# Stores of the early stages issued by GpSimd instead of SyncE in a one-core encoder layer

## The chip, the cores and the metric

The kernel runs on one core of a Trainium2 chip. A core has a tensor engine (TensorE, PE in the profile), a vector engine (VectorE, DVE), a scalar engine (ScalarE, ACT), GpSimd (POOL) and SyncE (SP), which here does nothing but issue transfers. Each engine runs its own instructions in order, and they wait for each other through semaphores. Transfers between the core's memory and the chip's large memory are carried by 16 DMA engines; an engine that issues a transfer writes it into its own queue and goes on, and whoever needs the data waits for its landing. The metric is the time of one execution in microseconds on the device, as the median of several.

## The reference

One layer of a bidirectional encoder, batch 1, 1024 rows, width 2048, in fp32:

```
mod = silu(c) @ w_ada + b_ada;  shift, scale, gate = split(mod, 3)
h = rmsnorm(x, pre_g) * (1 + scale) + shift
q, k, v, gate_a, u, gate_p = split(h @ w_in)           # 1024, 256, 256, 1024, 1024, 1024 columns
y_a = windowed_gqa(q, k, v, rel_table, sink) * silu(gate_a)   # 8 heads of 128, window of 128
y_p = multiscale_pool(u, w_grp, scale) * silu(gate_p)         # 4 groups, windows 2, 4, 8, 16
g_a, g_p = split(sigmoid(h @ w_merge + b_merge))
merged = g_a * (y_a @ w_br_attn) + g_p * (y_p @ w_br_pool)
out = x + gate * rmsnorm(merged @ w_out, post_g)
```

## The kernel before, in words

Every large product is fp32, made of three products of halves: ACT rounds a tile to its high part (`whi`, L96) and VectorE subtracts that to get the low part (`wlo`, L97). On top of that `strassen` (L213 on) saves one product in eight: a block of 2x2 tiles is computed with seven products, named by their moving operands B11, T3, T2, B21, T4, T1, B22, into three PSUM banks X, Z and V (TensorE's L238). Each product is 12 matmuls. Its weight halves live in rings of four tiles, so weights are prepared up to four products ahead. The seventh product of a block runs after the first two of the next block's. The results of a block are called c (two tiles), u2 and p7; the tiles named `ev` or `part` they stand in are free again once the store that reads them has landed. A block's inner dimension is done in two halves, and the sums of the first half travel through the large memory.

The stages, in order of time:

- Start-up, to about 60 us: x is normalized and turned, and parts of `w_ada` come in, column by column, for shift and scale.
- The ramp: five blocks over smaller pieces of the inner dimension. The first of them is written as a plain product (`plain_block`, stores at L665 into `ramp_d0`). Their results go to `ramp_d` and come back as `part` (L210).
- Pass one, the first half of the inner dimension for `w_in` and `w_merge`: c, u2 and p7 are stored to `part_d` by `to_dram` (L315). Beside it run sums of weights for the last stage (`weight_sums`: loads `sw` at L795, sums on VectorE, stores to `ws_d` at L807), the lines of the attention's bias (`bias_lines`, L828 to L838: `oh`, `line_d`, `bias_d`, always issued by GpSimd) and the gate's row (`pg_d`, L867).
- Pass two, the second half: parts are loaded from `part_d` (L210), added, and the results stored to `proj_d` (L315). Beside it run the attention (loads of `qr`, `kvr`, `g` from `proj_d`, stores of `ya_d` at L1085) and the pooling (`yp_d`, L1177).
- The merge: two branches b = 0 and b = 1, eight blocks each. Branch 0 stores its results to `mp_d` (L1306); branch 1 adds them and stores `m_d` (L1311). The gate tiles `gt` come from `proj_d` (L1271).
- The output projection with row tiles of its own; first row tiles are stored by GpSimd (`o_d` at L1443, `out_dram` at L1371 through `first_rows`), the last ones by SyncE (`finish_block`, L1371).

The order of instructions on each engine is set by a scheduler that works from its own estimates, except where `keep` pins an instruction to its place in the program. Before the change SyncE's one queue holds the loads and 445 stores, in one order: a store whose result isn't ready yet holds up every load behind it. A queue has eight transfers under way at most, since it uses eight completion semaphores in turn.

Two names of the code are touched: `load` and `store`, set side by side, and the default of `finish_block`.

Of the kernel before, what the change touches and what calls it, by code (L numbers as in the profile page):

```python
# [43 lines left out]
def encoder_layer(ctx: ExitStack, tc: tile.TileContext, x, c, table, w_ada, b_ada, pre_g,  # L44
# [15 lines left out]
    nc = tc.nc  # L60
# [30 lines left out]
    def keep(ins):  # L91

        tc.keep_in_program_order(ins)
# [12 lines left out]
        return nc.vector.tensor_tensor(o, a, b, ALU.subtract)  # L106

    load = nc.sync.dma_start
    store = nc.sync.dma_start

    ident = const.tile([P, P], F32, name="ident")
    make_identity(nc, ident)
# [243 lines left out]
    for r0, src in ((0, c[0]), (16, b_ada[0, 0:D]), (32, b_ada[0, D:2 * D]),  # L356
                    (48, pre_g[0]), (64, b_merge[0]), (96, pool_scale[0])):
        n = src.shape[0] // P
# [996 lines left out]
    def rows_of(T, n):  # L1355
        return out[T * P:(T + 1) * P, n * 512:(n + 1) * 512]
# [8 lines left out]
        nc.vector.reciprocal(s_[:, 2:3], s_[:, 1:2])  # L1365
        return s_[:, 2:3]

    def finish_block(T, n, scale, store=store):
        r = held.pop((T, n))
        keep(nc.vector.scalar_tensor_tensor(r, r, scale, xrow.pop((T, n)), op0=ALU.mult, op1=ALU.add))  # L1370
        store(rows_of(T, n), r)  # L1371
# [11 lines left out]
    def out_pair(half, i, op, between, after=None):  # L1383
# [101 lines left out]
        for t in range(2):  # L1485
            for j, w in enumerate(ws):
                out_mm(bz[t], op, "B22", j, t, w, False, j == len(ws) - 1)
            result("12", t, bz[t], c12[t])
            scale = row_scale(6 + t)
            for n in (0, 2, 3, 1):  # L1490
                finish_block(6 + t, n, scale)
# [7 lines left out]
    def first_rows(T, n):  # L1499

        def place(name):
            ring.rotate(-1)
            return ring[-1]

        def fetch():
            if (T, n) not in held:
                held[T, n] = place("fo")
                keep(load(held[T, n], o_d[T * P:(T + 1) * P, n * 512:(n + 1) * 512]))
            fetch_x_block(T, n, place)

        def put_out():
            if T not in scales:
                scales[T] = row_scale(T)
            finish_block(T, n, scales[T], nc.gpsimd.dma_start)

        return fetch, put_out
# [53 lines left out]
    def third_block():  # L1570
        assert not side
        for T in (4, 5):
            scale = row_scale(T)
            for b in range(4):
                finish_block(T, b, scale)
# [43 lines left out]
```

## Time and profile before

| | |
|---|---|
| median of three executions | 2119.83 us (2118.78 to 2121.57) |
| the profiled execution | 2119.98 us, span 2118.2 us |
| TensorE busy, granted clock | 2083.7 us, 98% of the span; 0.997 |
| VectorE, ACT, GpSimd busy | 1541.5 us (73%), 1108.4 us (52%), 20.1 us (1%) |
| moved by SyncE's queue | 457.82 MB, 66.1% of the time of 16 DMA engines |
| moved by GpSimd's queue | 8.48 MB, 1.0% |

The page gives the busy time of each engine and the chain of work that ended last. A row of the view of waits names the engine, its operation and source line, then the engine that released it; after the colon stand the microseconds in total, how often, and the longest. A row of the timeline gives the start, the length, the engine, line and tiles. A row of the view of busy time by stretch gives the stretch, its length, the busy time of TensorE (and how many instructions), of its weight loads, of VectorE, ACT and GpSimd, the granted clock, the share of the DMA engines and GB/s. `SPq` is SyncE's sequencer. A row of DMA issues ends with the size in KB and the median time from issue to landing.

### The profile page before, as it was taken

The numbers are of one execution on the slowest core, as the hardware profiler recorded it, in microseconds if no ns is written. First come the engines' busy times: TensorE is split into PE (matmuls) and PEld (weight loads), VectorE is DVE, ScalarE is ACT, GpSimd is POOL, SyncE is SP. The second block draws the span as 40 slices with busy tenths as digits, with TensorE's granted clock in tenths as the row PEclk, the third lists the DMA queues.
The fourth block names the chain that finished last, engine by engine and source line by source line (L and its number), as shares of the span: only waits on it lengthen the run. The fifth ranks groups of instructions, "written<-read, shape, count | busy, mean of one in ns | idle before, by whom it ended". The sixth has DMA issues, their size and how long they took to land.

```text
span 2118.2 us, 29001 instructions
## 1 busy us (share of the span) xinstructions
PE 2083.7 (98%) x9573; PEld 1715.9 (81%) x9573; DVE 1541.5 (73%) x2767; ACT 1108.4 (52%) x2106; POOL 20.1 (1%) x90
## 2 busy tenths in 40 slices
PE   6999999999999999999999999999999999999998
PEld 4688888888887888888888888888888788888886
DVE  5787667777546776677777678866957977889667
ACT  4654444444366544665656544333645645768654
POOL 0000000000000000000000000000000000000000
PEclk9999999999999999999999999999999999999999
DMA  9887656899767456544645476676745566786896
GB/s 332 276 267 229 204 190 212 290 307 324 252 194 238 148 178 200 169 159 161 198 145 168 154 240 226 211 225 197 250 155 173 173 195 197 225 307 218 299 342 214
DMA packets 302934, 468.20 MB, mean 221 GB/s; under 512 B 24074, under 2 KB 145058, under 8 KB 302784
## 3 DMA queue, kind: packets, MB, share of 16 engines
q1 hardware_dynamic: 299408, 457.82, 66.1%
q0 software_dynamic: 3040, 8.48, 1.0%
q8 instruction: 75, 1.23, 0.2%
q14 instruction: 75, 0.61, 0.1%
q10 hardware_dynamic: 336, 0.06, 0.0%
HBM read 341.45 MB, written 126.90 MB: 221 GB/s over the span
## 4 chain that ended last, share of the span: by engine, by line
PE 92%; DVE 4%; DMA 3%; issue 1%; ACT 0%; SPq 0%; ACTq 0%; DVEq 0%
PE Z L238 31%; PE X L238 20%; PE V L238 20%; PE Z L1349 2%; PE Z L1351 2%; PE Z L1350 2%; PE X L1351 1%; PE X L1349 1%; PE X L1350 1%; PE V L1349 1%; PE V L1351 1%; PE V L1350 1%; DMA ada<-in_w_ada_dram 1%; PE PT L1060 1%; DVE wlo L97 1%; DMA xt<-in_x_dram 1%
## 5 line engine op out<-in xcount | busy, mean ns | idle before, releaser
L96 ACT ACTIVATE whi<-raw 128x512 fp32r<-128x512 f32 (+1 forms) x532 | 322.0, 606 | 515.9 <-PE Z L238 255.1
L97 DVE TENSOR_TENSOR wlo<-raw,whi 128x512 fp32r<-128x512 f32 (+1 forms) x532 | 347.1, 657 | 164.7 <-PE Z L238 125.2
L97 DVE TENSOR_TENSOR wlo<-wr,whi 128x512 fp32r<-128x512 f32 x224 | 151.3, 689 | 56.5 <-ACT whi L96 51.1
L96 ACT ACTIVATE whi<-wr 128x512 fp32r<-128x512 f32 x224 | 138.9, 629 | 89.0 <-DVE wlo L97 37.2
L103 DVE TENSOR_TENSOR raw<-raw,raw 128x512 f32<-128x512 f32 x79 | 54.6, 691 | 104.5 <-DMA raw<-in_w_merge_dram 78.8
L238 PE MATMUL V<-T3h,whi 128*128 128x512 f32 x334 | 91.4, 392 | 1.5 <-DVE u L103 1.0
L96 ACT ACTIVATE whi<-ws 128x512 fp32r<-128x512 f32 (+1 forms) x88 | 53.5, 608 | 74.5 <-PE X L238 68.2
L238 PE MATMUL Z<-T2h,whi 128*128 128x512 f32 x334 | 91.1, 392 | 0.5 <-ACT whi L96 0.5
L238 PE MATMUL X<-B11h,whi 128*128 128x512 f32 x334 | 91.3, 392 | 0.0
L238 PE MATMUL Z<-T1h,whi 128*128 128x512 f32 x334 | 91.3, 391 | 0.0
L238 PE MATMUL Z<-T2h,wlo 128*128 128x512 f32 x334 | 90.3, 390 | 1.0 <-DVE wlo L97 1.0
L238 PE MATMUL Z<-B22h,whi 128*128 128x512 f32 x334 | 91.1, 392 | 0.0
L238 PE MATMUL V<-T4l,whi 128*128 128x512 f32 x334 | 90.7, 390 | 0.3 <-DVE T4l L97 0.2
L238 PE MATMUL X<-B21h,whi 128*128 128x512 f32 x334 | 90.7, 391 | 0.0
L238 PE MATMUL V<-T3l,whi 128*128 128x512 f32 x334 | 90.4, 390 | 0.2 <-DVE T3l L97 0.2
L238 PE MATMUL V<-T4h,whi 128*128 128x512 f32 x334 | 90.6, 391 | 0.0
L238 PE MATMUL Z<-T1l,whi 128*128 128x512 f32 x334 | 90.4, 390 | 0.1
L238 PE MATMUL X<-B11l,whi 128*128 128x512 f32 x334 | 90.4, 390 | 0.0
L238 PE MATMUL X<-B11h,wlo 128*128 128x512 f32 x334 | 90.3, 390 | 0.0
L238 PE MATMUL Z<-T1h,wlo 128*128 128x512 f32 x334 | 90.2, 390 | 0.0
L238 PE MATMUL Z<-B22l,whi 128*128 128x512 f32 x334 | 90.2, 390 | 0.0
L238 PE MATMUL X<-B21l,whi 128*128 128x512 f32 x334 | 90.2, 389 | 0.0
(353 smaller groups left out, 4838.3 us busy)
## 6 DMA issues: line engine op xcount, KB each, us to landing
part<-part_d SPq DMA_DIRECT2D x136, 256.0 KB, 4.7
ada<-in_w_ada_dram SPq DMA_DIRECT2D x128, 256.0 KB, 5.3
raw<-in_w_merge_dram SPq DMA_DIRECT2D x64, 512.0 KB, 5.5
wr<-ws_dS SPq DMA_DIRECT2D x64, 512.0 KB, 5.3
raw<-in_w_in_dram SPq DMA_DIRECT2D x62, 512.0 KB, 4.1
wr<-in_w_out_dram SPq DMA_DIRECT2D x48, 512.0 KB, 5.6
proj_d<-part SPq DMA_DIRECT2D x68, 256.0 KB, 2.2
sw<-in_w_out_dram SPq DMA_DIRECT2D x64, 256.0 KB, 5.8
```

What stands on the lines that cost most here:

```text
L96: ins = (nc.scalar.activation(hi, src, AF.Copy), nc.vector.tensor_tensor(lo, src, f32(hi), ALU.subtract))
L97: nc.vector.tensor_tensor(lo, src, f32(hi), ALU.subtract))
L103: return (eng or nc.vector).tensor_tensor(o, a, b, ALU.add)
L238: nc.tensor.matmul(ps, w_[:, i], op[mov][j][m_], start=fresh and i == 0 and n == 0, stop=i == nj - 1 and n == 2, skip_group_check=True)
L1060: nc.tensor.transpose(pt[:, i * P:(i + 1) * P], p[:, i * P:(i + 1) * P], ident)
L1349: nc.tensor.matmul(pb, hi, w[0], start=first, stop=False, skip_group_check=True)
L1350: nc.tensor.matmul(pb, lo, w[0], start=False, stop=False, skip_group_check=True)
L1351: nc.tensor.matmul(pb, hi, w[1], start=False, stop=last, skip_group_check=True)
```

## The change

The name `store`, which all stages use, becomes GpSimd's issue instead of SyncE's; `finish_block` keeps SyncE as its default.

```
@@ -106,7 +106,7 @@
     load = nc.sync.dma_start
-    store = nc.sync.dma_start
+    store = nc.gpsimd.dma_start
@@ -1365,7 +1365,7 @@
-    def finish_block(T, n, scale, store=store):
+    def finish_block(T, n, scale, store=nc.sync.dma_start):
```

So 429 stores leave SyncE's queue for GpSimd's: those at L315, L665, L807, L867, L1085, L1177, L1306 and L1311. GpSimd issues 456 transfers afterwards instead of 27. Every load that reads stored rows, and every tile that is reused after a store, still waits for the landing. The scheduler also places some instructions of the other engines anew: on TensorE it is 104 lines of difference in 9185 rows, the largest of which puts the products T2 and B21 of the block with bank Z_5318 ahead of its T3.

In the rows below a number behind a name tells buffers apart. First SyncE at the end of the start-up, before: `ada` are pieces of `w_ada`, `raw` weights of `w_in`, `ramp_d` with L665 the four stores of the plain block.

```order
L665 DMA ramp_d_86<-c_781 128x512
L471 DMA ada_413<-in_w_ada_dram 128x2x256
L188 DMA raw_415<-in_w_in_dram 128x2x256 x2
L188 DMA raw_418<-in_w_in_dram 128x2x256 x2
L665 DMA ramp_d_86<-c_786 128x512
L665 DMA ramp_d_86<-c_799 128x512
L665 DMA ramp_d_86<-c_804 128x512
L315 DMA ramp_d_87<-c_880 128x512
```

The same place on SyncE after the change:

```order
L471 DMA ada_411<-in_w_ada_dram 128x2x256
L471 DMA ada_413<-in_w_ada_dram 128x2x256
L188 DMA raw_415<-in_w_in_dram 128x2x256 x2
L188 DMA raw_418<-in_w_in_dram 128x2x256 x2
L188 DMA raw_1242<-in_w_in_dram 128x2x256 x2
L188 DMA raw_1245<-in_w_in_dram 128x2x256 x2
L188 DMA raw_1248<-in_w_in_dram 128x2x256 x2
L210 DMA part_1391<-ramp_d_87 128x512
```

The stores are gone from between the loads. On GpSimd they follow its last fill of a tile in the start-up:

```order
L549 MEMSET B22l_385 128x1
L665 DMA ramp_d_86<-c_781 128x512
L665 DMA ramp_d_86<-c_786 128x512
L665 DMA ramp_d_86<-c_799 128x512
L665 DMA ramp_d_86<-c_804 128x512
L315 DMA ramp_d_87<-c_880 128x512
```

All four stand there in a row, with nothing but their own results to wait for.

Second, GpSimd around the bias lines, before (`tab` is the table that `oh` selects from):

```order
L549 MEMSET B22l_385 128x1
L828 MEMSET tab 33x8
L831 DMA oh<-in_onehot_dram 33x512
L836 DMA line_d<-bl 8x512
L837 DMA bias_d<-line_d 1024x1x512
```

And after, from the store that stands ahead of `oh`:

```order
L315 DMA part_d<-p_1040_4836 128x512
L831 DMA oh<-in_onehot_dram 33x512
L836 DMA line_d<-bl 8x512
L315 DMA part_d<-c_5030 128x512
L837 DMA bias_d<-line_d 1024x1x512
L315 DMA part_d<-c_5084 128x512
L315 DMA part_d<-u_1080_5055 128x512
L315 DMA part_d<-p_1070_4997 128x512
L315 DMA part_d<-c_5199 128x512
L807 DMA ws_dS_98<-sw_5090 128x512
L315 DMA part_d<-c_5251 128x512
L807 DMA ws_dS_97<-sw_5202 128x512
```

The three transfers now stand among stores of pass one and of the weight sums.

Third, SyncE some 20 us later, before: `sw` are the loads for the weight sums, `xt` the last row tiles of x.

```order
L795 DMA sw_5259<-in_w_out_dram 128x512
L795 DMA sw_5261<-in_w_out_dram 128x512
L795 DMA sw_5263<-in_w_out_dram 128x512
L795 DMA sw_5265<-in_w_out_dram 128x512
L315 DMA part_d<-c_5199 128x512
L188 DMA raw_5381<-in_w_merge_dram 128x4x256
L315 DMA part_d<-c_5251 128x512
L315 DMA part_d<-u_1112_5233 128x512
L188 DMA raw_5383<-in_w_merge_dram 128x4x256
```

And after:

```order
L795 DMA sw_5259<-in_w_out_dram 128x512
L795 DMA sw_5261<-in_w_out_dram 128x512
L188 DMA raw_5381<-in_w_merge_dram 128x4x256
L188 DMA raw_5383<-in_w_merge_dram 128x4x256
L188 DMA raw_5565<-in_w_merge_dram 128x4x256
L795 DMA sw_5263<-in_w_out_dram 128x512
L795 DMA sw_5265<-in_w_out_dram 128x512
L188 DMA raw_5567<-in_w_merge_dram 128x4x256
L919 DMA xt_5539<-in_x_dram 128x512
```

Three loads of weights have moved ahead of the second half of the `sw` loads.

## The prediction

> **What bounds the kernel now.** I read the page first, its busy line and its chain of waits, and then TensorE's own waits.
>
> ```profile
> PE 2083.7 (98%) x9573; PEld 1715.9 (81%) x9573; DVE 1541.5 (73%) x2767; ACT 1108.4 (52%) x2106; POOL 20.1 (1%) x90
> PE 92%; DVE 4%; DMA 3%; issue 1%; ACT 0%; SPq 0%; ACTq 0%; DVEq 0%
> ```
>
> TensorE is busy for 98% of the span and carries 92% of the chain. A queue matters only where it makes TensorE stand. The view of busy time by stretch says how much standing there is after the start-up:
>
> ```profile
> 60.00:100.00 40.00, 37.20 (x190) 22.88 (x189) 30.18 (x68) 25.45 (x53) 0.00 (x0) 1.00 0.88 288
> 100.00:2080.00 1980.00, 1975.76 (x9025) 1640.85 (x9025) 1448.49 (x2556) 1036.91 (x1949) 16.50 (x44) 1.00 0.66 217
> ```
>
> Between 60 and 100 us TensorE stands 2.80 us, between 100 and 2080 us 4.24 us. So 7.0 us is the most that quicker loads could give back; the last 38 us keep their stores on SyncE. Nothing of that size limits a loss. Next, what SyncE's queue waited for:
>
> ```profile
> SPq L315 <- DVE part L103: 225.0, 53, 11.2
> SPq L315 <- ACT c L310: 177.1, 52, 7.1
> ```
>
> The two costliest rows are 402 us in which a store stood at the head of SyncE's queue for a result, with loads queued behind it. That is what the change takes away. It looks large, but only 7.0 us of standing was ever TensorE's.
>
> **The price of a store.** The change moves 429 stores, nearly all of 128x512 floats, to GpSimd. GpSimd already issues some of the same shape, so both prices stand in the trace (the view by source line, then the DMA issues with microseconds from issue to landing):
>
> ```profile
> L1371 POOL DMA_DIRECT2D out_dram<-mo x8: 539/540/542, 2014.0 to 2050.5; - x8
> L1371 SPq DMA_DIRECT2D out_dram<-mo x8: 332/332/351, 2096.6 to 2113.3; - x8
> ...
> proj_d<-part SPq DMA_DIRECT2D x68, 256.0 KB, 2.2
> mp_d<-c SPq DMA_DIRECT2D x16, 256.0 KB, 2.0
> out_dram<-mo POOLq DMA_DIRECT2D x8, 256.0 KB, 5.7
> out_dram<-mo SPq DMA_DIRECT2D x8, 256.0 KB, 2.3
> out_dram<-c POOLq DMA_DIRECT2D x2, 256.0 KB, 7.0
> oh<-in_onehot_dram POOLq DMA_DIRECT2D x1, 66.0 KB, 3.3
> ```
>
> Issue: 429 x 0.54 = 232 us of GpSimd, which is idle but for 20.1 us, so it costs nothing by itself. SyncE gets 429 x 0.33 = 142 us back, also free. Landing is what counts: 5.7 against 2.3 us, 3.4 us more for each store. I use 6 us for a landing from GpSimd. Whoever waits for a landing sees it later: a buffer that is reused, or a load that reads the stored rows back. Most have cover, because weights are prepared up to four products ahead and a product of 12 matmuls is 2.7 us (three groups of four that start 0.91 us apart; two of them, 802.97 to 804.78, stand under term 5). I walked the changed order against the times of before, looking for waits whose cover is under 3.4 us.
>
> [...]
>
> **Term 1, the head.** Up to 83 us the transfers are the bound. ACT has the four ramp_d0 tiles ready by 66.4 us, SyncE issues their stores between its loads, and VectorE then stands 6 us for the weight tile raw:
>
> ```profile
> L664 ACT ACTIVATE c<-PB x4: 595/601/608, 63.2 to 65.8; 128x512 f32<-128x512 f32 x4
> L665 SPq DMA_DIRECT2D ramp_d<-c x4: 319/338/343, 75.4 to 81.2; - x4
> 76.91 2.60 SPq L188 DMA_DIRECT2D raw<-in_w_in_dram  x4
> 79.81 1.68 SPq L665 DMA_DIRECT2D ramp_d<-c  x3
> DVE ws L106 <- DMA raw<-in_w_in_dram: 6.0, 1, 6.0
> 72.00:76.00 4.00, 4.00 (x26) 1.90 (x25) 1.48 (x4) 1.20 (x3) 0.00 (x0) 1.00 1.10 347
> 80.00:84.00 4.00, 3.45 (x22) 1.97 (x21) 1.02 (x3) 1.01 (x2) 0.00 (x0) 1.00 1.10 380
> ```
>
> Before, one of the four stores is ahead of raw and three are behind it. After, GpSimd has nothing else to do and issues all four at 64 to 67 us, so three more stores, 786 KB, pass the full engines before raw. At 347 GB/s that is 2.3 us; the mixed stretch ran at 380, which makes it a little less. If stores rode along wholly free it would be 0. I take +2.0, near the upper end, because 380 is nearer to 347 than to a rate that would carry them free. VectorE's sum behind raw moves by that, and TensorE, which already stands there (3.45 of 4 us busy), with it.
>
> **Term 2, the bias lines.** Before, GpSimd's queue holds these three alone. Afterwards the one-hot load oh stands behind a store of the seventh product, which is ready at 532.8 us:
>
> ```profile
> 532.81 0.32 SPq L315 DMA_DIRECT2D part_d<-p  x1
> 526.93 0.66 POOL L831 DMA_DIRECT2D oh<-in_onehot_dram  x1 [364.69 <-DMA raw<-in_w_merge_dram]
> 545.67 1.11 POOL L837 DMA_DIRECT2D bias_d<-line_d  x1 [5.08 <-DMA line_d<-bl]
> 538.12 1.02 PE L833 MATMUL b<-oh,tab 33*8 33x512 f32 x2
> ```
>
> oh leaves at 532.8 + 0.5 = 533.3 us and lands 3.3 us later, at 536.6, which is 1.5 us ahead of TensorE's use; if it takes a store's 6 us, TensorE waits 1.2. I take +0.5 (0 to 1.5). bias_d waits in GpSimd for line_d's landing, 5.1 us, with nine or more stores queued behind; they go out late by that, and stores of weight sums also wait behind one of ACT's c.
>
> **Term 3, the weight sums and the last row of x, 555 to 602 us.** In the changed order the loads sw_5263 and sw_5265 stand behind raw_5565. Before, they left in the burst of four that began at 554 us; raw_5565 left at 582.7:
>
> ```profile
> 554.13 8.91 SPq L795 DMA_DIRECT2D sw<-in_w_out_dram  x4
> 582.70 4.04 SPq L188 DMA_DIRECT2D raw<-in_w_merge_dram  x2
> 580.51 1.28 SPq L919 DMA_DIRECT2D xt<-in_x_dram  x3
> 583.75 1.34 ACT L920 ACTIVATE xt<-xt,rstd 128x512 f32<-128x512 f32 x2 [1.50 <-DMA xt<-in_x_dram]
> 600.59 0.60 PE L926 MATMUL b<-ident,xt 128*128 128x128 f32 x4
> sw<-in_w_out_dram SPq DMA_DIRECT2D x64, 256.0 KB, 5.8
> ```
>
> Step by step: sw at 583.2, landed at 589.0 (5.8); two sums on VectorE of 0.7 each, 590.4; the store from GpSimd landed at 596.4; xt reuses that buffer, loads 3.2 us as here (580.51 to 583.75), 599.6; scaled 0.7 later, 600.3. TensorE transposes xt at 600.6. So the 17 us of cover (583.75 to 600.59) are used up, and what is left is 0 to 2 us; I take +0.9. ACT stands some 6 us for it, but the next weights are not used before 603 us.
>
> **Term 4, the turn between the two branches.** c must be stored before ACT may write the seventh product's copy into its buffer:
>
> ```profile
> 1650.08 0.32 SPq L1306 DMA_DIRECT2D mp_d<-c  x1
> 1653.89 0.60 ACT L248 ACTIVATE p<-V 128x512 f32<-128x512 f32 x1 [0.23 <-PE V L238]
> 1658.42 0.61 ACT L96 ACTIVATE T4h<-y 128x512 fp32r<-128x512 f32 x1
> 1659.13 1.07 PE L238 MATMUL V<-T4h,whi 128*128 128x512 f32 x4
> 1640.00:1660.00 20.00, 20.00 (x88) 16.27 (x88) 19.87 (x34) 15.76 (x29) 0.00 (x0) 1.00 0.43 143
> ```
>
> Before it lands at 1652.1 (2.0 us), after at 1656.1: ACT is 2.2 us late. Behind it stand the four T4h, the last of which ends 0.1 us before the product that reads it begins, and VectorE, 19.87 of 20 us busy, cannot catch up. Bounds 0 to 2.2; I take +1.5, since the fourth tile is read last.
>
> **Term 5, the rest.** The first query tile is read back as soon as its rows are stored:
>
> ```profile
> 789.58 0.32 SPq L1010 DMA_DIRECT2D qr<-proj_d  x1
> 792.78 0.62 ACT L1015 ACTIVATE qhi<-qr 128x512 fp32r<-128x512 f32 x1
> 802.97 1.07 PE L238 MATMUL X<-B21h,whi 128*128 128x512 f32 x4
> 804.78 1.07 PE L238 MATMUL X<-B21h,wlo 128*128 128x512 f32 x4
> ```
>
> The stored rows had landed at 789.6; with 4 us more it is 793.6, so ACT is 4 us late at 796.8. The weights behind it on ACT are those of the product at 802.97, wanted with their low part at 804.78; that leaves 6 us for 4, and this is hidden. A dozen such turns have less cover each; +0.6 for all (0 to 4). Gains: loads that no longer queue behind stores, -0.4, at most -7.0 by the standing time above.
>
> **Sum:** 2.0 + 0.5 + 0.9 + 1.5 + 0.6 - 0.4 = +5.1 us. The profiled execution took 2119.98 us in all, 0.15 more than the median 2119.83, so the median becomes 2119.83 + 5.1 = 2124.9 us.
>
> **The rivals.** *Faster:* SyncE's freed queue sends weights and parts earlier, and the landings are all covered. For it: the 402 us above. Against: TensorE stands only 7.0 us, part of it for VectorE and ACT. If half is recovered, 2116.3 us; it decides when more than 4.2 of the 7.0 come back.
>
> *Everything hidden:* the ring of four products absorbs terms 2 to 4, and the head's stores ride along: 2120.5 us. For it: most loads have 4 us of cover and more.
>
> *The software queue backs up:* 456 issues in 2118 us are one per 4.6 us. Two stores of c from GpSimd landed at a median of 7.0 us. If the first took the 5.7 of the others, the second took 8.3, 2.6 more; a bunch of four would then end at 13.5 us, and the pool of six tiles runs short. Each pass-one pair of weight sums, 16 of them, losing 0.7 us gives +11 us with the terms above at half: 2134 us. It decides when a store in a bunch lands later than about 9 us. [...]
>
> **Chances.** The forecast's neighbourhood, 2122 to 2129: 0.56. All hidden, 2118 to 2122: 0.22. Backed up, above 2129: 0.15. Faster than 2118: 0.07. The range from 2118 to 2135 leaves out about 0.07 below and 0.08 above. By 0.2%, 4.2 us, about what a measurement can tell from no change, the line between "same" and "slower" is 2124.1, inside the forecast's own neighbourhood: I give it 0.35 slower and 0.21 same. With the others: faster 0.06, same 0.43, slower 0.51.
>
> **What would show it.** Right: VectorE's wait for raw before 90 us rises from 6.0 to about 8; landings of proj_d and part_d from GpSimd near 6 us; ACT waiting for a landing of mp_d near 1656 us; xt scaled at about 600 us. Wrong: TensorE's standing time after 100 us staying at 4 us (all hidden), or growing by tens of us at the weight sums (backed up).

## The result, and the profile after

The changed kernel takes 2175.54 us (median of five, 2173.97 to 2179.35) against 2121.57 us (2118.78 to 2123.80) for the kernel before on the same chip: a ratio of 1.0261, with a 95% interval of 1.025 to 1.0272. It is 54 us slower, where 5 us were forecast. The profiled execution took 2179.35 us, with a span of 2177.6 us and a mean granted clock of 0.987.

The busy line and the chain of waits of the changed kernel:

```profile
PE 2104.5 (97%) x9573; PEld 1727.2 (79%) x9573; DVE 1541.4 (71%) x2767; ACT 1108.6 (51%) x2106; POOL 252.0 (12%) x519
PE 75%; issue 10%; DMA 8%; DVE 4%; POOL 1%; ACT 1%; SPq 0%; DVEq 0%; POOLq 0%; ACTq 0%
```

This execution is the slowest of the five. Its span is 59.4 us longer than that of the kernel before, in two parts. TensorE stands 2177.6 - 2104.5 = 73.1 us where it stood 34.5: 38.6 us more. And it is busy 2104.5 us where it was 2083.7, with the same 9573 matmuls: 20.8 us more for the same work. VectorE and ACT do what they did, in the same time. GpSimd's added issues make it busy for 252.0 instead of 20.1 us; no wait of TensorE's is put down to it.

The view of busy time by stretch says where. First the changed kernel:

```profile
100.00:400.00 300.00, 299.86 (x1341) 247.99 (x1340) 213.99 (x367) 137.15 (x243) 43.52 (x81) 1.00 0.68 224
400.00:730.00 330.00, 296.68 (x1280) 238.76 (x1279) 184.91 (x274) 136.88 (x275) 61.58 (x113) 0.95 0.69 227
730.00:1230.00 500.00, 499.15 (x2442) 422.57 (x2441) 358.70 (x784) 283.66 (x596) 59.81 (x111) 1.00 0.53 171
1230.00:1450.00 220.00, 214.24 (x955) 176.38 (x954) 165.64 (x305) 84.63 (x145) 25.43 (x61) 0.98 0.63 199
```

and of the kernel before the two stretches of pass one that answer to the second row:

```profile
408.00:545.00 137.00, 137.00 (x602) 112.16 (x601) 101.39 (x144) 56.65 (x95) 1.18 (x2) 1.00 0.93 314
545.00:650.00 105.00, 103.50 (x498) 85.66 (x497) 51.26 (x80) 57.98 (x132) 1.11 (x1) 1.00 0.68 221
```

In the second half of pass one TensorE lacks 33 of 330 us, and its clock is 0.95. That place was full before: from 408 to 545 us TensorE worked for 137.00 of 137 us, and the DMA engines were busy for 93% of it. Pass two, 730 to 1230 us, lost nothing.

To see it more finely I paired each matmul of the changed kernel with the same one of before and took how much later it runs. Times are those of the kernel before; the figures are worked out from the two traces. They serve for all runs below. (In the runs of one store group alone, whole blocks near 600 us change places, so there only the figures up to 529 and from 1171 us on are safe.)

| us later at | 127 | 408 | 529 | 569 | 649 | 1171 | 1411 | 2093 |
|---|---|---|---|---|---|---|---|---|
| changed kernel | 4.1 | 4.1 | 31.3 | 38.8 | 52.0 | 52.2 | 62.3 | 60.7 |
| ramp and attention back (e5) | -0.2 | -0.2 | 20.9 | 29.3 | 45.4 | 45.8 | 46.8 | 46.9 |
| pass one back (e9) | 4.0 | 4.0 | 4.5 | 4.5 | 3.3 | 4.2 | 7.7 | 7.4 |
| sums of weights back (e1) | 4.8 | 4.8 | 18.4 | 26.6 | 39.8 | 39.8 | 49.8 | 49.5 |
| side loads on GpSimd too (e11) | 4.0 | 4.0 | 14.8 | 28.7 | 41.2 | 43.4 | 50.2 | 49.9 |
| side loads paced (e12) | 3.0 | 3.0 | 15.5 | 25.2 | 38.0 | 38.8 | 47.3 | 48.2 |
| sum last (e6) | 3.2 | 2.9 | 2.8 | 6.6 | 20.2 | 20.4 | 26.0 | 29.0 |
| sum last, sums back (e13) | 2.9 | 2.6 | 2.5 | 7.0 | 18.4 | 18.1 | 27.3 | 29.3 |
| sum last, much back (e8) | 1.3 | 1.0 | 1.0 | 7.5 | 18.6 | 18.5 | 20.3 | 23.1 |
| before, sum early (e7) | 0.3 | 0.4 | 5.1 | 5.1 | 5.9 | 5.3 | 5.5 | 5.2 |
| before, sums' stores alone (e2) | 1.0 | 1.0 | 11.5 | | | 44.2 | 44.0 | 43.9 |
| before, results' stores alone (e10) | 0.7 | 0.7 | 17.3 | | | 49.3 | 49.6 | 49.2 |

So the changed kernel's 60.7 us are 4.1 at the head, 27.2 from 408 to 529 us, 7.5 around the bias lines, 13.2 up to 649 us, 0.2 in pass two up to 1171 us, 10.1 in the attention, and 1.6 given back.

What TensorE waited for, over the whole of the changed kernel, and what VectorE waited for:

```profile
PE V L238 <- DVE u L103: 23.8, 8, 5.5
PE b L926 <- ACT h L929: 6.1, 3, 3.1
PE b L833 <- issue: 4.3, 1, 4.3
PE Z L238 <- ACT u L292: 3.3, 1, 3.3
...
DVE ws L106 <- DMA raw<-in_w_merge_dram: 54.5, 15, 10.2
```

In the kernel before the first and the last of these rows read:

```profile
PE V L238 <- DVE u L103: 1.0, 1, 1.0
...
DVE ws L106 <- DMA raw<-in_w_merge_dram: 24.9, 10, 4.9
```

TensorE's product T3 waits for VectorE's `u`. That is u2, a result of block n that takes over bank V; the bank has to be empty before T3 of the next block may write it. And VectorE was waiting for a weight load. One such place, VectorE first, then TensorE:

```profile
458.02 0.69 DVE L97 TENSOR_TENSOR wlo<-ws,whi 128x512 fp32r<-128x512 f32 x1
468.88 0.69 DVE L106 TENSOR_TENSOR ws<-raw 128x512 f32<-128x512 f32 x1 [10.18 <-DMA raw<-in_w_merge_dram]
469.49 0.68 DVE L103 TENSOR_TENSOR u<-V,u 128x512 f32<-128x512 f32 x1
...
463.62 1.07 PE L238 MATMUL X<-B11h,wlo 128*128 128x512 f32 x4
470.23 2.08 PE L238 MATMUL V<-T3h,whi 128*128 128x512 f32 x4 [5.54 <-DVE u L103]
472.10 1.91 PE L238 MATMUL V<-T3l,whi 128*128 128x512 f32 x4
473.81 1.37 PE L238 MATMUL V<-T3h,wlo 128*128 128x512 f32 x4
475.02 1.09 PE L238 MATMUL Z<-B22h,whi 128*128 128x512 f32 x4
```

VectorE has nothing wrong with it but its place in line: next in its order is `ws`, the sum of weights that a product of the block after next will need (L265), and its source hasn't landed. For 10.18 us VectorE stands. The very next instruction is u2, which takes 0.68 us and which TensorE needs now; TensorE stands 5.54 us. Then the three groups behind the wait start 1.87, 1.71 and 1.21 us apart instead of 0.91, so the wait costs some 2.1 us more. The granted clock of that place (the 0.50 near the end of the row) says why:

```profile
468.00:472.00 4.00, 1.77 (x4) 1.48 (x5) 3.12 (x6) 0.00 (x0) 0.00 (x0) 0.50 0.02 6
```

The trace records ten such stretches at half clock between 60 and 2100 us of the changed kernel, twelve periods of 3.41 us in all, and none there in the kernel before. TensorE works 37.1 us in them; by the granted clock of 0.50 that would be 18.5 us less at full clock (my estimate), which is most of the 20.8 us by which it is longer busy. 10.4 of these 18.5 us stand behind waits for `u` (six of its eight waits lie between 400 and 573 us). The length of a wait alone doesn't tell them apart: the wait of 5.54 us had half clock behind it, and so had waits of 1.90 us (1366 to 1368 us) and 2.12 us (492 to 494 us), while one of 2.82 us (443 to 445 us) had not. The clock's records in this trace begin whole periods of 3.41 us apart, and what fits the changed kernel after 100 us is how much of one such period is lost: with 1.9 us or more of standing in a period, the next was at half clock; with 1.66 us or less, as in each of the two periods that the wait of 2.82 us lay across (1.16 and 1.66 us), a period at full clock was never followed by one at half.

The order was the kernel's, not the data's. Here are VectorE's rows as the two kernels hold them, one block earlier than the rows above (u2_886 empties bank V). Before:

```
L103 TENSOR_TENSOR u2_886_4055<-V_867_3961,u2_886_4055 128x512
...
L97 TENSOR_TENSOR wlo_928_4269<-raw_882_4033,whi_927_4268 128x512
L106 TENSOR_TENSOR ws_937_4316<-raw_915_4200 128x512
```

and after:

```
L106 TENSOR_TENSOR ws_937_4316<-raw_915_4200 128x512
L103 TENSOR_TENSOR u2_886_4055<-V_867_3961,u2_886_4055 128x512
...
L97 TENSOR_TENSOR wlo_928_4269<-raw_882_4033,whi_927_4268 128x512
```

The weight sum moved ahead by sixteen places, past u2. The diff moves no instruction of VectorE; the scheduler did. Why it chose so isn't shown.

The other half is the load. SyncE's issues around one such load (raw_882, the last `raw` in both), of the changed kernel and then of the kernel before:

```profile
403.72 4.26 SPq L795 DMA_DIRECT2D sw<-in_w_out_dram  x2
408.04 1.91 SPq L820 DMA_DIRECT2D gada<-in_w_ada_dram  x4
411.44 0.38 SPq L188 DMA_DIRECT2D raw<-in_w_merge_dram  x1
```
```profile
402.84 0.43 SPq L820 DMA_DIRECT2D gada<-in_w_ada_dram  x1
405.32 0.33 SPq L315 DMA_DIRECT2D part_d<-c  x1
405.69 0.44 SPq L188 DMA_DIRECT2D raw<-in_w_merge_dram  x1
406.17 0.61 SPq L820 DMA_DIRECT2D gada<-in_w_ada_dram  x1
407.15 0.38 SPq L188 DMA_DIRECT2D raw<-in_w_merge_dram  x1
```

Before, the stores of results stood between the side loads (`gada`, 512 KB each) and spread them, since each waited for its result: from 385 to 412 us SyncE stood 16.3 us for results to store, and from 387 to 425 us the `gada` left 2.5 to 8.3 us apart. With the stores gone, the four `gada` of a block leave in one bunch, within 1.91 us here, just ahead of the weight load on which VectorE waits.

### The profile page after: what moved, and what is told of

Read it like the earlier page. It is cut to its first block, busy times and chain, and to the rows that moved or that the text cites. A ratio compares the mean times of both kernels' runs of the same rounds, so it can differ in the third digit from the quotient of the medians.

```text
span 2177.6 us, 29394 instructions
## 1 busy us (share of the span) xinstructions
PE 2104.5 (97%) x9573; PEld 1727.2 (79%) x9573; DVE 1541.4 (71%) x2767; ACT 1108.6 (51%) x2106; POOL 252.0 (12%) x519
## 4 chain that ended last, share of the span: by engine, by line
PE 75%; issue 10%; DMA 8%; DVE 4%; POOL 1%; ACT 1%; SPq 0%; DVEq 0%; POOLq 0%; ACTq 0%
PE Z L238 24%; PE V L238 16%; PE X L238 16%; DMA raw<-in_w_merge_dram 2%; DMA xt<-in_x_dram 2%; PE Z L1349 2%; PE Z L1351 2%; PE Z L1350 2%; DMA ada<-in_w_ada_dram 2%; PE X L1350 1%; PE V L1350 1%; PE X L1351 1%; PE X L1349 1%; PE V L1349 1%; PE V L1351 1%
## 5 line engine op out<-in xcount | busy, mean ns | idle before, releaser
L96 ACT ACTIVATE whi<-raw 128x512 fp32r<-128x512 f32 (+1 forms) x532 | 322.2, 607 | 546.5 <-PE Z L238 252.0
L96 ACT ACTIVATE whi<-wr 128x512 fp32r<-128x512 f32 x224 | 139.3, 629 | 88.3 <-DVE wlo L97 38.8
L238 PE MATMUL V<-T3h,whi 128*128 128x512 f32 x334 | 94.6, 402 | 24.6 <-DVE u L103 23.8
L106 DVE TENSOR_TENSOR ws<-raw 128x512 f32<-128x512 f32 (+1 forms) x88 | 58.4, 664 | 74.0 <-DMA raw<-in_w_merge_dram 54.5
L238 PEld LDWEIGHTS V<-T3h,whi 128*128 128x128 f32 x334 | 62.2, 191 | 40.5 <-DVE u L103 25.2
L238 PE MATMUL V<-T3h,wlo 128*128 128x512 f32 x334 | 93.0, 399 | 0.0
L238 PE MATMUL Z<-B22h,wlo 128*128 128x512 f32 x334 | 91.4, 394 | 0.0
L238 PE MATMUL Z<-T2l,whi 128*128 128x512 f32 x334 | 91.3, 393 | 0.0
L238 PE MATMUL V<-T4h,wlo 128*128 128x512 f32 x334 | 90.2, 389 | 0.3 <-DVE wlo L97 0.3
```

The source lines that it names most:

```text
L96: ins = (nc.scalar.activation(hi, src, AF.Copy), nc.vector.tensor_tensor(lo, src, f32(hi), ALU.subtract))
L238: nc.tensor.matmul(ps, w_[:, i], op[mov][j][m_], start=fresh and i == 0 and n == 0, stop=i == nj - 1 and n == 2, skip_group_check=True)
```

## The experiments

In the expectations, theory A is that SyncE stands for the ring of weight sums (loads `sw` waiting for a `ws_d` store to land), so that weight loads leave late; theory B is that GpSimd's queue as a whole is too slow; theory C is VectorE's order. The letter D stands for two things: in the runs on VectorE's order, that loads are late whatever the order; in the run with the side loads paced, that more bytes under way make the load late.

**Which stores.** Five runs put a group of stores back, or move one group alone.

Sums of weights back, in the changed kernel:

```
-                store(ws_rows(name)[:, j, i * 512:(i + 1) * 512], t)
+                nc.sync.dma_start(ws_rows(name)[:, j, i * 512:(i + 1) * 512], t)
```

> Only the 64 stores of the weight sums go back to SyncE; the other 365 moved stores stay on GpSimd. Theory A: from 408 to 650 us of the time of before, SyncE's loads of sw wait for landings of weight-sum stores that stand in GpSimd's queue behind stores of results, and weight loads stand behind those sw loads; then the 48 us lost there fall below 10, the 4 us of the head and the 9 us after 1170 us stay, and the time is 2133 us (2128 to 2142). Theory B: GpSimd's queue as a whole is too slow for all stores of pass one, whatever they are; then more than 25 of the 48 us stay, 2158 us or more.

Measured 2165.55 us, ratio 1.0206 (1.0183 to 1.0229). From 408 to 649 us 35 of 48 us remain, as theory B expected, so the ring of weight sums isn't the main thing.

The same line the other way round, in the kernel before (only these stores moved):

> The kernel before, with only the 64 stores of the weight sums moved to GpSimd. Theory A: most of the 48 us comes back, 2150 to 2170 us. Theory B: GpSimd's queue has only 64 stores more and nothing stands ahead of them, so there is little, below 2126 us. In between: it takes both, the stores on GpSimd and the result stores ahead of them there.

Measured 2164.28 us, 1.0204 (1.0189 to 1.022): here theory A's range, not B's. These 64 of the 429 moved stores give 44 of the 54 us. VectorE's order turns here too, and TensorE waits for u2 (8.3 us in all). But only 10.5 of the 43.9 us are lost from 408 to 529 us. Much of the rest is lost where the last row tiles of x are turned: from 680 to 740 us of that run TensorE works 44.8 of 60 us at a granted clock of 0.80, standing for ACT's `xt` above all.

The results of pass one alone (`part_d`), in the kernel before:

```
-            run(strassen(w, n0, rows_in_turn(0), range(4), op, ev, to_dram(block(part_d, ORDER[i])),
+            run(strassen(w, n0, rows_in_turn(0), range(4), op, ev, to_dram(block(part_d, ORDER[i]), store=nc.gpsimd.dma_start),
```

> The kernel before, with only the result stores of pass one (part_d) on GpSimd, the weight sums' on SyncE. VectorE has ws ahead of u2 at four to six blocks of that stretch, where the kernel before has u2 first. Theory C with loads that leave SyncE unpaced: 20 to 40 us lost there, 2140 to 2160 us. If the loss needs the weight sums' stores on GpSimd: below 2126 us.

Measured 2169.33 us, 1.0226 (1.021 to 1.0242), 9 us above the range of theory C. Here too 16.6 of the 48.5 us behind the head are lost by 529 us, and TensorE stands for `xt` later on. Either group alone costs nearly what all stores together cost, though not in the same places; the costs of the groups don't add up.

All stores of pass one back on SyncE (`part_d`, `ws_d`, `pg_d`), the rest as changed:

> The changed kernel with the stores of pass one (part_d, ws_d, pg_d) back on SyncE; those of the ramp, of pass two, of the attention, the pooling and the merge stay on GpSimd. If pass one is where the loss arises, and the stages don't act on each other: 4 us of the head and 9 us after 1170 us stay, 2133 us (2127 to 2138). If pass two on GpSimd costs more once pass one runs well, as the turn of the merge did in e6_sum_last: up to 2140 us.

Measured 2129.21 us (seven runs), 1.0036 (1.0024 to 1.0048). VectorE makes u2 ahead of the weight sum again. Between 408 and 649 us nothing is lost any more, and of TensorE's waits in pass one 0.2 us is left:

```profile
PE b L926 <- ACT h L929: 0.2, 1, 0.2
```

The other 248 stores on GpSimd (20 of them the ramp's into `part_d`) cost 9 us: the head (4 us) and the attention (3.5 us).

The first ramp block, the ramp's, the attention's and the pooling's stores (L665, L315 for the ramp's parts in `ramp_d` and `part_d`, L1085, L1177) back on SyncE, the rest as changed:

```
-                store(block(ramp_d[0], 0)(blk), t)
+                nc.sync.dma_start(block(ramp_d[0], 0)(blk), t)
...
-                    store(ya_d[h * P:(h + 1) * P, (j - 3) * P:(j + 1) * P], g[e])
+                    nc.sync.dma_start(ya_d[h * P:(h + 1) * P, (j - 3) * P:(j + 1) * P], g[e])
```

> The stores of the ramp (32) and of the attention and the pooling (24) go back to SyncE, the rest stays on GpSimd. If the head's 4 us come from ramp stores that pass the full engines ahead of raw, and the 4 us near 1207 us from the attention's last store, both go, and the 48 us of the weight sums stay: 2165 to 2169 us. If the head's loss has another cause, it stays: 2169 to 2177 us.

Measured 2166.78 us, 1.0219 (1.0202 to 1.0236). The head's 4.1 us are gone, and of the attention's 10.1 us 1.0 is left. VectorE waits for the head's `raw` as before the change, 5.9 us (8.5 in the changed kernel):

```profile
DVE ws L106 <- DMA raw<-in_w_in_dram: 5.9, 1, 5.9
```

**VectorE's order.** The changed kernel, with the weight sum of a block bound behind the low half of T1 on VectorE (a matter of order alone, no added wait between engines), only in pass one:

```
+                if part is None and nj == 4:
+                    behind(s3_ins, t1_low[0])
```

> The changed kernel, all stores as in it, but in pass one the weight sum ws of the next block is bound behind the low part of T1 on VectorE, where it stands in the kernel before; the changed order has it ahead of u2, so that VectorE waits there for a weight load. Theory C, VectorE's order: the 31 us lost from 408 to 569 us of the time of before fall below 8, the losses of the head, of 569 to 650 and after 1170 us stay, and the time is 2143 us (2133 to 2152). Theory D, the loads land too late in engines shared with GpSimd's stores, wherever the sum stands: 2162 us or more.

Measured 2146.59 us, 1.0129 (1.0114 to 1.0144). Of 27.2 us from 408 to 529 none is left, though two of the loads there landed as late as in the changed kernel (10.5 and 10.0 us, table below). TensorE's waits for u2 fall from 23.8 to 3.6 us, of which 3.0 are at the head:

```profile
PE V L247 <- DVE u L112: 3.6, 2, 3.0
```

The reverse, in the kernel before: the weight sum is made early and u2 bound behind it, in pass one; all stores stay on SyncE.

```
+        s3 = wp.tile([P, 4, P], F32, tag="ws", name=uid("ws"))
+        behind(last_u2[0], sub(s3, first[:, :, 0:P], first[:, :, P:2 * P]))
```

> The kernel before, all stores on SyncE, but in pass one u2 is bound behind the weight sum ws of the next block on VectorE, as the changed order has it. Theory C: VectorE now waits for loads ahead of u2 and TensorE for VectorE, 2145 to 2170 us with no store moved. Theory D: SyncE's loads land in time, and the time stays below 2126 us.

Measured 2124.55 us (ten runs), 1.0021 (1.0011 to 1.0032). The bad order alone costs 5 us, with one wait of 2.9 us near 484 us, where theory C expected 25 us or more. So both halves are needed: the early place, and a load that is late. With both the stretch loses 27 us, with the one 5, with the other none.

**Why the load is late.** Side loads off SyncE's queue, to see whether `raw` is late because it stands behind them. First the `sw` loads on GpSimd too:

```
-                load(a[name], wo_rows(kh)[:, j, n0:n0 + 512])
+                nc.gpsimd.dma_start(a[name], wo_rows(kh)[:, j, n0:n0 + 512])
```

> As the changed kernel, and the 64 loads of sw go to GpSimd too, so that no weight load on SyncE stands behind a load that waits for a landing. Theory A: VectorE's waits for raw in that stretch fall back to those of before and the time is 2130 to 2145 us, though the weight-sum stores land no earlier. Theory B: no gain, 2165 us or more, since GpSimd's queue has even more to do.

Measured 2172.77 us, 1.0246 (1.0223 to 1.0268). The intervals of this run and the changed kernel overlap: no gain is shown.

Then `sw` and `gada` on GpSimd:

```
-            keep(load(st_["at"], w_ada[kc * P:(kc + 1) * P, 2 * D + q * 1024:2 * D + (q + 1) * 1024]))
+            keep(nc.gpsimd.dma_start(st_["at"], w_ada[kc * P:(kc + 1) * P, 2 * D + q * 1024:2 * D + (q + 1) * 1024]))
```

> The changed kernel with the loads of sw and of gada on GpSimd too, so that SyncE has little but weight loads in pass one, while VectorE keeps ws ahead of u2. If a weight load lands late because SyncE's queue has sent sw and gada right ahead of it: its landing falls from 8 to 10 us to some 6, and the time to 2150 us or less. If it lands late because it shares the engines with GpSimd's queue: landings and time stay, 2168 us or more.

Measured 2171.67 us, 1.0243 (1.022 to 1.0266). Whole-kernel times say no. The table says more: 408 to 529 us loses 10.8 instead of 27.2 us, and the stretch behind it, up to 649 us, 26.4 instead of 20.7 us. The first two weight loads of the stretch still take 10.6 and 8.8 us to land (10.3 and 9.8 in the changed kernel), the next two 7.1 and 6.8 (8.2 and 7.1). So here a landing was long without side loads on SyncE's queue. But the gain in the first stretch says that the queue has some part: SyncE stands there for no store of weight sums any more (38.2 us from 408 to 573 us in the changed kernel).

That led to the last theory: what makes the landing long is how many bytes are under way ahead of `raw`, on either queue. To test it, each `gada` load in the changed kernel waits for the last result made before it, as it did indirectly when that result's store stood ahead of it on SyncE. Two of the four then stand behind `raw`; VectorE's order for u2 and the weight sum stays the bad one.

```
+            tc.add_manual_dep(ins.ins, last_result[0].ins.name,
+                              mybir.DependencyInfo(mybir.DependencyClass.Sync, mybir.DependencyReason.DATA),
...
-            keep(load(st_["at"], ...
+            keep(paced(load(st_["at"], ...
```

> The changed kernel, but each load of the gate's weights (gada) waits for the last result of the product before it, the one whose store stood ahead of such loads on SyncE's queue in the kernel before. VectorE's order stays that of the changed kernel (weight sum ahead of u2); two of the four gada loads of a block now stand behind the weight load raw instead of ahead of it, and 1 MB less is in flight when raw leaves. Theory D (the load lands late because more bytes are in flight ahead of it, the stores having paced the loads before): the landings of 8.4 to 10.3 us of raw's first halves fall to about 7, u2 is held for 0 to 3 us, and of the 31 us lost over the stretch of 408 to 569 us (times of before) at most 15 remain, the median falls from 2175.5 to 2150 to 2162. Rival (two queues share the transfer engines, so that a load takes longer beside GpSimd's stores, however many loads go ahead of it): landings and loss stay, 2168 to 2178.

Measured 2164.90 us, 1.0202 (1.0185 to 1.0219): 2.9 us above the upper end expected of theory D, and below the rival's range. Between 408 and 529 us 12.5 of 27.2 us are left (up to 569 us, with the bias lines, 22.2 of 34.7, where 15 were expected). TensorE's waits for u2, 23.8 us in the changed kernel:

```profile
PE V L247 <- DVE u L103: 16.0, 7, 4.8
```

Below are the four loads that the weight sums of 408 to 500 us wait for, in KB still under way on both queues when the load leaves (counting each transfer as moving evenly from issue to landing, an estimate of mine from the trace, rough to some 0.3 MB, since some landings aren't recorded) and us from issue to landing. The column of the run with the sum last shows the changed kernel's transfers under VectorE's old order.

| load | before | changed | sum last | side loads paced |
|---|---|---|---|---|
| raw_882 | 1368, 7.2 | 1826, 10.3 | 1856, 10.5 | 1254, 7.2 |
| raw_915 | 1404, 7.7 | 2057, 9.8 | 2016, 10.0 | 970, 5.3 |
| raw_949 | 1143, 7.8 | 1596, 8.2 | 1413, 8.9 | 1193, 7.7 |
| raw_982 | 1141, 8.1 | 1067, 7.1 | 1723, 13.2 | 1161, 7.7 |

Landings tend to follow the bytes: below 1.4 MB they took 5.3 to 8.1 us, above 1.8 MB 9.8 to 10.5 us. In between they lie between 7.7 and 13.2 us, so this is a tendency, not a rule. With side loads paced these landings are as short as before. (The other weight load of each block pays for it: 7.1 to 10.7 us, where the changed kernel has 6.4 to 9.9.) So here the bunch made the landing long (10.3 and 9.8 us for the first two loads, 7.2 and 5.3 with the side loads paced), and taking it apart gives back about half the loss. For the other half the load leaves late. SyncE's waits in that run from 408 to 573 us:

```profile
SPq L804 <- DMA ws_dS<-sw: 36.9, 11, 9.6
SPq L197 <- DVE wlo L97: 33.7, 10, 9.5
```

In the changed kernel these are 38.2 and 36.8 us; in the kernel before, from 408 to 545 us, they are 2.5 and 4.9. SyncE stands for stores of weight sums to land, and for VectorE's `wlo`, which frees the weights' ring and is itself behind the stalled VectorE. As I read it, VectorE's stall delays the load that makes its next stall; blocks of the changed kernel take 24 us where they took 19. No run tests this loop, and what share each of the two waits has wasn't separated.

**The stretch behind, 569 to 649 us.** It still loses 13.6 us in the run with the sum last. The first load of x (`xt`) waits there 6.4 us for a sum's store to land. To test that, the run with the sum last with the `ws_d` stores on SyncE again:

> The changed kernel with the weight sum bound behind T1's low half, as in the run e6_sum_last, and with the stores of the weight sums for the output projection (ws_d) on SyncE again; the results' stores stay on GpSimd. In e6_sum_last 17 us were lost between 545 and 680 us, where the first load of x (xt) waits for a weight sum's store from GpSimd to land. If that landing is the cause (term 3 of the prediction, with a larger size), xt leaves earlier, that loss falls to 5 to 9 us, and the median from 2146.6 to 2134 to 2140. If the loss there comes from elsewhere (bias lines, loads that are late for another reason, results of pass one), 2143 to 2150.

Measured 2151.29 us, 1.0142 (1.0126 to 1.0157): 1.3 us above the rival's range, and far from the theory's. `xt` still waited 4.7 us for a landing, so the wait was shortened, not taken away. But the first `xt` left at 586.9 us instead of 604.4 and nothing was gained, since the turning of x now came earlier too. ACT stands for `xt`, and the copies that TensorE needs stand behind it:

```profile
595.34 0.72 ACT L933 ACTIVATE xt<-xt,rstd 128x512 f32<-128x512 f32 x1 [2.57 <-DMA xt<-in_x_dram]
597.39 0.72 ACT L933 ACTIVATE xt<-xt,rstd 128x512 f32<-128x512 f32 x1 [1.33 <-DMA xt<-in_x_dram]
598.02 0.58 ACT L323 ACTIVATE c<-X 128x512 f32<-128x512 f32 x1
...
598.65 2.07 PE L247 MATMUL V<-T3h,whi 128*128 128x512 f32 x4 [5.80 <-ACT c L323]
```

It is the same pattern on another engine: an instruction that waits for a load stands ahead of one that is ready.

**Together.** The run with the sum last, and the ramp's, attention's and pooling's stores and the bias load `oh` back on SyncE:

> As e6_sum_last, with the stores of the ramp, the attention and the pooling and the load of oh back on SyncE. If the losses of the stages add up, the head's 4 us, 3 of the 4 us of the attention and the 4 us of oh go as well: some 11 us less than e6_sum_last, 2132 us by theory C (2122 to 2141). If they don't add, since another wait takes their place, it is within 4 us of e6_sum_last.

Measured 2143.30 us, 1.0124 (1.0102 to 1.0146): 3.3 us less than with the sum last alone, and the two intervals overlap. The attention's loss goes (1.8 us left from 1171 to 1411 us), the bias wait doesn't: `oh` on SyncE now stands behind a weight load that waits for its buffer, and TensorE waits 4.3 us for it, as long as in the changed kernel.

No version tried is faster than the kernel before.

## Why the prediction was wrong

**The step that failed** is the one behind all five terms: "I walked the changed order against the times of before, looking for waits whose cover is under 3.4 us." It asked where a store lands later. It took for granted that loads land when they did, and that the other engines' orders, VectorE's above all, matter only where a store is waited for; of the other engines' orders, only TensorE's differences are counted under the change. Both were wrong. The 27.2 us from 408 to 529 us come from VectorE's new order (undone, nothing is lost there) together with a weight load that lands and leaves later; neither is in the sum. In the kernel before that stretch had no slack to see: 137.00 of 137 us on TensorE, DMA engines at 93%.

**The price of a store** was too high where it was thought to matter. "I use 6 us for a landing from GpSimd":

```profile
proj_d<-part POOLq DMA_DIRECT2D x68, 256.0 KB, 3.0
part_d<-c POOLq DMA_DIRECT2D x58, 256.0 KB, 4.3
ws_dS<-sw POOLq DMA_DIRECT2D x64, 256.0 KB, 5.7
mp_d<-c POOLq DMA_DIRECT2D x16, 256.0 KB, 3.7
oh<-in_onehot_dram POOLq DMA_DIRECT2D x1, 66.0 KB, 7.0
```

Against before this is 0.8 us more for `proj_d` (2.2), 1.8 for `part_d` (2.5), 1.5 for `ws_d` (4.2) and 1.7 for `mp_d` (2.0): about half the 3.4 us or less. The late landings of single stores were never the main cost. The 5.7 us on which the price rested were also true, but as the median of eight stores that left one by one near the end and took 3.4 to 7.5 us each.

**Term 1, the head, +2.0:** right in its mechanism, and short in size: 4.1 us. TensorE's wait itself grew from 1.0 to 3.5 us, near the 2.0 forecast; the rest is a period at half clock behind it (88.7 to 92.1 us), which the term left out. GpSimd issues all four stores by 68.2 us, ahead of `raw`, and VectorE's wait rose from 6.0 to 8.5 us, near the 8 foretold; the stores taken back, all of it is gone.

```profile
65.07 1.24 POOL L665 DMA_DIRECT2D ramp_d<-c  x2 [7.69 <-ACT c L664]
67.12 1.07 POOL L665 DMA_DIRECT2D ramp_d<-c  x2 [0.82 <-ACT c L664]
86.19 0.42 DVE L106 TENSOR_TENSOR ws<-raw 128x256 f32<-128x256 f32 x1 [8.55 <-DMA raw<-in_w_in_dram]
87.94 0.73 PE L238 MATMUL V<-T3h,whi 128*128 128x512 f32 x2 [3.54 <-DVE u L103]
```

**Term 2, the bias lines, +0.5:** right in place and mechanism (`oh` left right behind the store of the seventh product), mis-sized. A load of 66 KB took 7.0 us to land, beyond the 6 I allowed, and TensorE waited 4.3 us, against a bound of 1.5:

```profile
566.98 0.54 POOL L831 DMA_DIRECT2D oh<-in_onehot_dram  x1
574.07 1.86 PE L833 MATMUL b<-oh,tab 33*8 33x512 f32 x2 [4.33 <-issue]
```

With two periods at half clock behind it (573.4 to 580.2 us) the stretch lost 7.5 us.

**Term 3, weight sums and x, +0.9:** right that `xt` would wait for a sum's landing and use up its cover; the place lost 13.2 us. The cover was reckoned from the old times of the sums, and these were already late. The run with the sums' stores back on SyncE shortened that wait and gained nothing, so what the landing is worth here stays open.

**Term 4, the turn between the branches, +1.5:** in the changed kernel ACT waited 0.7 us for the landing and nothing was lost (61.1 us late at 1640 us, 60.7 at 2093). In the runs with the sum last the mechanism is there as foretold: ACT waits 2.5 to 3.4 us for the landing of `mp_d`, TensorE 2.1 to 3.0 us behind it, and 3.0 to 4.3 us are lost between 1640 and 2093 us. Of the run with the sum last and stores back:

```profile
1673.64 0.60 ACT L257 ACTIVATE p<-V 128x512 f32<-128x512 f32 x1 [2.53 <-DMA mp_d<-c]
1674.80 2.08 PE L247 MATMUL Z<-T2h,whi 128*128 128x512 f32 x4 [2.13 <-ACT whi L96]
```

**Term 5, the rest, +0.6 (0 to 4):** 10.1 us, nearly all in the attention from 1171 to 1411 us, 9.1 of them gone when the stores of ramp, attention and pooling were put back together. TensorE stands there 2.4 us for `g`, 1.9 for VectorE's `u` and 1.2 for ACT's, with two periods at half clock (from 1262.9 and from 1368.7 us); which store is behind each wait wasn't traced. **Gains, -0.4:** none to be seen; 402 us less of standing stores on SyncE gave back nothing.

**The clock** wasn't a term at all. Slower matmuls made 20.8 of the 59.4 us, 18.5 of them in the periods at half clock that followed ten of the waits.

**The rivals.** "Backed up" had the place, the weight sums of pass one, and the sign that TensorE's standing grows by tens of us. Its range, above 2129 us, is the one that came, but its time of 2134 us was 41 us short, and its mechanism fell: GpSimd's queue didn't run late (the groups of 256 KB landed at medians of 2.7 to 6.5 us, and 3 of the 429 moved stores took over the 9 us that it needed), the two stores on which its step of 2.6 us rested took 6.4 and 7.6 us in the kernel before, and moving still more work onto that queue (`sw`, `gada`) changed the time by no more than 4 us, to the better. GpSimd's issues of the moved stores took 0.54 us in the median, as the prediction counted, and 0.77 us at most. The faster rival and the hidden one failed with the forecast, since stores on an in-order queue weren't only in the way; they also spaced the loads.

## What to carry to other kernels

Moving transfers off a queue changes when the ones that stay will leave: here stores that waited for their results, 402 us in the two costliest rows, paced the loads behind them, and without them four side loads left within 1.91 us ahead of the one load that was urgent. Before costing the moved instructions, compare the order on every in-order engine before and after, and look for an instruction that waits for a load and now stands ahead of one that the busiest engine needs. What a late load costs hangs on that order: here loads that landed in some 10 us cost nothing from 408 to 529 us with u2 first, and were part of a loss of 27.2 us with the weight sum first.

## What was not expected of the hardware

Stores of 128x512 floats from GpSimd landed in 2.7 to 6.5 us by the medians of their groups (`ya_d` and a group of `o_d`), where the eight of the kernel before showed 5.7; no single price fits them.

The stall of 5.54 us on TensorE, up to 470.23 us, cost some 2.1 us more in slower matmuls behind it, and the stall of 1.90 us near 1367 us was followed by a period of 3.41 us at half clock.

The time to land of the four 512 KB loads of the table, in four runs, tended to grow with what was under way ahead of them by my estimate: 5.3 to 8.1 us with 1.0 to 1.37 MB, 9.8 to 10.5 us with 1.8 to 2.1 MB, and 7.7 to 13.2 us in between. With `sw` and `gada` on the other queue the first two of these loads still took 10.6 and 8.8 us.
